# A two-layer decoder trunk: output projections one token half at a time, and the first MLP iteration's activations made product by product

## Chip, cores and metric

One core of one Trainium2 chip runs the whole program. The metric is device time in microseconds (us) of that core, from one execution; the median over three executions is compared. A profiled execution gives the trace that is read here.

## The reference

Two layers, each a mixer and an MLP, on 1024 tokens of width 1024 in fp32. What matters of it:

```python
# layer 0
y = concat([ssd_mixer(...), diff_attention(...)]) @ e_w_out      # 2048 -> 1024
# layer 1
y = concat([retention(...), sliding_window_attention(...)]) @ o_w_out   # 1536 -> 1024
def squared_relu_mlp(h, w1, w2):
    return square(relu(h @ w1)) @ w2                             # 1024 -> 4096 -> 1024
def sandwich(x, c_act, sublayer, g_pre, g_post, w_mod, b_mod):
    shift, scale, gate = split(c_act @ w_mod + b_mod, 3)
    h = rms_norm(x, g_pre) * (1 + scale) + shift
    return x + gate * rms_norm(sublayer(h), g_post)
```

Each layer runs `sandwich` twice, with the mixer and with the MLP. The normalisation is over a whole token row, so a token's `post` (gate, norm, residual) and the next `pre_norm` can begin only when every group of input columns has been projected for that token.

## The kernel before

**Numbers.** Each fp32 operand is split into a high part (a cast on ScalarE, line 156 for weights) and a low part (source minus high part, on VectorE, line 158). A product of two split operands is three matmuls: high by high, high by low, low by high. So every unit below is a run of triples of 128x512 matmuls on TensorE.

**Queues.** The program is written with tile pools, and a timeline scheduler sets the order of instructions on each engine from the order in the code, the buffers and its own estimates. Each engine then works strictly in that order: an instruction that waits holds up all that stand behind it. Weights arrive by DMA in `raw` (two buffers); the split parts `wh` and `wl` have four buffers each. `load_group` fetches one group of an output weight, 512 rows, as two 1 MB transfers and splits it into four blocks. Between them `bg` takes `bg_n` entries of a queue of background tasks (`bgq`): the modulation vectors of later sublayers, each a chain of four 1 MB loads and eight accumulations `macc` (line 299) on VectorE.

**Output projection.** `MixerOut` multiplies the mixer's result, which lies in DRAM (`yd`) by groups of 512 columns, with the output weight: four groups in layer 0, in the order 0, 1, 2, 3 (the first two SSD heads, the last two attention heads), and three in layer 1, in the order 2, 0, 1. Tokens come as 8 tiles of 128; tiles 0 to 3 are half 0, tiles 4 to 7 half 1. `half` loads a half group (`yr`), transposes it (`pyt`, four transposes for each of four blocks of 128 columns) and splits it (`u`). `out_unit` is one token tile by one 512-column half (`cc`) of the output: 12 matmuls (lines 466 to 468) into a bank `pg`, which VectorE then copies or adds into `Y` (lines 473 and 475). There are 8 units, 96 matmuls, in a half group.

The constructor runs half 0 of the first two groups while the second mixer of the layer (attention) goes on; `finish` then runs the rest. Before: half 1 of the second group, whose weights are still there, half 1 of the first group with its weights loaded again, and then each further group with both halves in one go. In the last group every tile's two units are followed by `post`, the `pre_norm` of the tile before, and from tile 5 on by `hT_cols` of half 0: the transposes `pht` that give the MLP its input, feature by token. The scheduler may bring rows of `finish` forward into the attention's last heads, which use the same engines: a block of 128 queries there goes score matmuls (`psc`) on TensorE, bias and row maximum on VectorE (line 1225), exponential on ScalarE, a weighted difference on VectorE (1238), transposes of the probabilities (`pat`, 1245), copies (1247), products with v (`pav`, 1251) and a normalisation (1255 to 1258).

**MLP.** `mlp` is a seven-product scheme over 2x2 blocks of the activations (half 0 and half 1 of the tokens, lower and upper 512 features) and of the weights. Each of eight iterations takes 256 columns of each weight half and runs products 1, 2, 4, 6, 7, 5, 3, each for two 128-column parts `g`, 12 matmuls (lines 557 to 559) per part. Products 1 and 2 use half 0 alone. In iteration 0, `second_half` turns half 1 (the transposes at line 574), makes the sums and differences and splits them, one quarter k after the other for all of products 4, 6, 7, 5, 3. `yp.whole` keeps half 0 in unsplit fp32 for it.

Of the kernel before, what the change touches and what calls it, by code (L numbers as in the profile page):

```python
# [9 lines left out]
F32 = mybir.dt.float32  # L10
F32R = mybir.dt.float32r
BF16 = mybir.dt.bfloat16
AF = mybir.ActivationFunctionType
# [15 lines left out]
def trunk(ctx: ExitStack, tc: tile.TileContext, x, c, rel_bias, norm_gains, mod_w, mod_b, mlp_w1, mlp_w2,  # L29
# [447 lines left out]
    def out_group(yp, us, blks, s, first, last):  # L477
        if not last:
            for cc in range(2):
                for t in range(NT):  # L480
                    out_unit(yp, us, blks, t, cc, first)
        else:
            xs = {}
            for t in range(NT):
                for cc in range(2):
                    out_unit(yp, us, blks, t, cc, first)
                xs[t] = post(yp, t, s)
                if s == sub_last:
                    continue
                if t:  # L490
                    pre_norm(yp, t - 1, xs[t - 1])
                if t == 5:
                    hT[0] = new_hT(0)
                    yp.whole = None
                    if s % 2 == 0:
                        pairs = [slot(17 + i, [P, 2, 512], F32, "whole") for i in range(3)]
                        pairs.append(const.tile([P, 2, 512], F32, tag="macc", name="whole"))
                        yp.whole = [t[:, i] for t in pairs for i in range(2)]
                if t >= 5:
                    k0 = (t - 5) * 3  # L500
                    hT_cols(yp, 0, s + 1, hT[0], range(k0, min(k0 + 3, 8)), yp.whole)
            if s != sub_last:
                pre_norm(yp, 7, xs[7])

                def second():
                    hT[1] = make_hT(yp, 1, s + 1)
                return second

# [4 lines left out]
    def mlp(yp, s):  # L513
# [19 lines left out]
        with ExitStack() as st:  # L533
# [27 lines left out]
            def second_half():  # L561
                a, b = mcol[s]
# [3 lines left out]
                for i, at_ in ((6, 8), (5, 4), (3, 0)):  # L566
                    A[i] = (of(pieces(at_)), of(pieces(at_ + 2)))
                for k in range(4):
                    a11, a12 = yp.whole[k], yp.whole[k + 4]
                    a2 = []  # L570
                    for kk, tag in ((k, "u3"), (k + 4, "c21")):
                        ps = pt.tile([P, 512], F32, tag="t", name="pht")
                        for i in range(4):
                            nc.tensor.transpose(ps[:, i * P:(i + 1) * P], yp.Y[4 + i][:, kk * P:(kk + 1) * P], ident)
                        a2.append(block(tag))
                        nc.scalar.activation(a2[-1], ps, AF.Identity, scale=a[:, kk:kk + 1], bias=b[:, kk:kk + 1])
                        if kk >= 4:
                            nc.scalar.activation(hh1[:, kk], ps, AF.Identity, scale=a[:, kk:kk + 1], bias=b[:, kk:kk + 1])
# [32 lines left out]
            for it in range(8):  # L611
# [11 lines left out]
                if it == 0:  # L623
                    second_half()
# [969 lines left out]
```

## Time and profile before

| what | value |
|---|---|
| median of 3 runs | 3029.69 us (3027.28 to 3030.26) |
| the profiled execution's own time | 3030.93 us |
| its span, first to last instruction | 3029.1 us |
| mean granted TensorE clock | 0.986 |
| TensorE busy | 97% of the span |
| VectorE busy | 66% |
| ScalarE busy | 43% |

The profiled execution took 1.24 us more than the median, and 1.8 us of its time lie outside the span. TensorE is busy nearly throughout, so the table alone says that few microseconds can be won; where its gaps are has to be read by place. Busy shares of the other engines are averages over stages that differ.

### The profile page before, as it was taken

To read this page: it belongs to the slowest core of one execution; us is meant where nothing else is said; L and a number is where in the kernel's file an instruction comes from. 1 tells how busy PE (TensorE), PEld (TensorE's weight loads), DVE (VectorE), ACT (ScalarE), POOL (GpSimd) and SP (SyncE) were. 2 spreads that over 40 slices of the span, in tenths; PEclk is the share of its full clock that TensorE was granted. 3 is DMA by queue.
4 is the path that set the end of the run, shared out by engine and by line. 5 is a ranking of instruction groups with operands and counts; after the bars stand their busy time and mean duration, and the time that the engine had idled before them with its cause. 6 is when DMAs were issued, how large, how long until landed. Compare 5 with 4: busy or idle time off the path is not lost.

```text
span 3029.1 us, 40060 instructions
## 1 busy us (share of the span) xinstructions
PE 2929.4 (97%) x15250; PEld 2471.4 (82%) x15250; DVE 1991.2 (66%) x3222; ACT 1309.4 (43%) x2348; POOL 474.2 (16%) x430
## 2 busy tenths in 40 slices
PE   8999999999999989999999989999999899999998
PEld 5888879888877867888888878989988678888887
DVE  5787885565586579876646845565454876666476
ACT  5232334555553264454433545432222644454333
POOL 0243443323210030000000232011101200000021
PEclk9999999999999999999999999999999999999999
DMA  6221311212142236646736542153242454476464
GB/s 215 75 89 57 120 53 46 66 41 61 46 150 71 89 127 217 221 163 235 290 125 226 191 134 63 33 168 101 84 153 77 140 188 162 153 260 231 151 223 166
DMA packets 268707, 413.59 MB, mean 137 GB/s; under 512 B 15337, under 2 KB 151138, under 8 KB 267618
## 3 DMA queue, kind: packets, MB, share of 16 engines
q1 hardware_dynamic: 268128, 410.92, 40.3%
q8 instruction: 120, 1.97, 0.3%
q14 instruction: 73, 0.60, 0.1%
q10 hardware_dynamic: 386, 0.11, 0.0%
HBM read 319.23 MB, written 91.75 MB: 136 GB/s over the span
## 4 chain that ended last, share of the span: by engine, by line
PE 81%; DVE 10%; DMA 4%; ACT 2%; issue 2%; POOL 1%; SPq 0%; POOLq 0%; DVEq 0%; ACTq 0%
PE pw L740 5%; PE pw L741 5%; PE pw L742 5%; PE pw L557 4%; PE pg L454 4%; PE pg L456 4%; PE pg L455 4%; PE pw L558 4%; PE pw L559 4%; PE pg L808 4%; PE pg L809 3%; PE pg L810 3%; PE pg L466 3%; PE pg L468 3%; PE pg L467 3%; PE pg L740 2%
## 5 line engine op out<-in xcount | busy, mean ns | idle before, releaser
L156 ACT CAST wh<-raw 128x1024 fp32r<-128x1024 f32 (+1 forms) x218 | 227.5, 1047 | 294.7 <-PE pw L558 97.7
L808 PE MATMUL pg<-wh,hh 128*128 128x256 f32 (+1 forms) x992 | 292.4, 295 | 18.5 <-DVE zs L843 10.6
L454 PE MATMUL pg<-hh,wh 128*128 128x512 f32 x736 | 292.8, 398 | 1.4 <-DVE ks L1340 0.8
L456 PE MATMUL pg<-hh,wl 128*128 128x512 f32 x736 | 291.9, 397 | 0.3 <-DVE ms L133 0.3
L455 PE MATMUL pg<-hl,wh 128*128 128x512 f32 x736 | 291.9, 397 | 0.0
L810 PE MATMUL pg<-wh,hl 128*128 128x256 f32 (+1 forms) x992 | 287.5, 290 | 0.6 <-DVE hl L439 0.6
L809 PE MATMUL pg<-wl,hh 128*128 128x256 f32 (+1 forms) x992 | 287.4, 290 | 0.0
L158 DVE TENSOR_TENSOR wl<-raw,wh 128x1024 fp32r<-128x1024 f32 (+1 forms) x162 | 199.3, 1232 | 130.3 <-ACT wh L156 127.4
L510 ACT CAST u<-uraw 128x1024 fp32r<-128x1024 f32 x112 | 117.1, 1049 | 299.8 <-PE pw L741 178.2
L511 DVE TENSOR_TENSOR u<-uraw,u 128x1024 fp32r<-128x1024 f32 x112 | 141.1, 1261 | 154.5 <-ACT u L510 153.7
L741 PE MATMUL pw<-wl,u 128*128 128x512 f32 x608 | 240.3, 395 | 0.0
L740 PE MATMUL pw<-wh,u 128*128 128x512 f32 x608 | 240.1, 396 | 0.0
L742 PE MATMUL pw<-wh,u 128*128 128x512 f32 x608 | 239.4, 394 | 0.0
L135 POOL TENSOR_TENSOR rs<-ms,expo 128x1 f32<-128x1 f32 x160 | 107.3, 671 | 682.2 <-DVE ms L133 664.2
L808 PEld LDWEIGHTS pg<-wh,hh 128*128 128x128 f32 x992 | 193.8, 195 | 21.9 <-DVE zs L843 10.3
L810 PEld LDWEIGHTS pg<-wh,hl 128*128 128x128 f32 x992 | 193.1, 195 | 2.5 <-DVE hl L439 1.3
L809 PEld LDWEIGHTS pg<-wl,hh 128*128 128x128 f32 x992 | 193.7, 195 | 1.8 <-issue 0.5
L466 PE MATMUL pg<-wh,u 128*128 128x512 f32 x448 | 181.9, 406 | 3.6 <-DVE u L940 3.1
L468 PE MATMUL pg<-wh,u 128*128 128x512 f32 x448 | 178.2, 398 | 0.0
L467 PE MATMUL pg<-wl,u 128*128 128x512 f32 x448 | 177.5, 396 | 0.0
L158 POOL TENSOR_TENSOR wl<-raw,wh 128x1024 fp32r<-128x1024 f32 x58 | 144.2, 2490 | 138.2 <-ACT wh L156 119.3
L454 PEld LDWEIGHTS pg<-hh,wh 128*128 128x128 f32 x736 | 139.1, 189 | 29.5 <-PE pg L456 1.2
(456 smaller groups left out, 7242.2 us busy)
## 6 DMA issues: line engine op xcount, KB each, us to landing
x<-in_mlp_w_dram SPq DMA_DIRECT2D x128, 512.0 KB, 6.6
uraw<-ud SPq DMA_DIRECT2D x56, 1024.0 KB, 5.5
raw<-in_mod_w_dram SPq DMA_DIRECT2D x24, 1024.0 KB, 5.0
ud<-sums SPq DMA_DIRECT2D x48, 512.0 KB, 4.2
raw<-in_mlp_w_dram SPq DMA_DIRECT2D x18, 1024.0 KB, 5.4
raw<-in_e_w_in_dram SPq DMA_DIRECT2D x32, 512.0 KB, 3.9
ud<-c SPq DMA_DIRECT2D x64, 256.0 KB, 3.1
mraw<-in_mod_w_dram SPq DMA_DIRECT2D x32, 512.0 KB, 4.9
```

Of the source, the lines that this page charges most:

```text
L158: lo_on[0].tensor_tensor(out=wl, in0=src, in1=wh.bitcast(F32), op=ALU.subtract)
L454: mm(ps, lhsT=wh[:, k], rhs=hh[:, k], start=(k == 0), stop=False)
L455: mm(ps, lhsT=wh[:, k], rhs=hl[:, k], start=False, stop=False)
L456: mm(ps, lhsT=wl[:, k], rhs=hh[:, k], start=False, stop=(k == 7))
L466: mm(ps, lhsT=uh[:, tl], rhs=wh[:, f % 2], start=(f == 0), stop=False)
L468: mm(ps, lhsT=ul[:, tl], rhs=wh[:, f % 2], start=False, stop=(f == 3))
L740: mm(ps[t], lhsT=uh[:, k, ts], rhs=wh[:, k], start=b, stop=False, **on)
L741: mm(ps[t], lhsT=uh[:, k, ts], rhs=wl[:, k], start=False, stop=False, **on)
L742: mm(ps[t], lhsT=ul[:, k, ts], rhs=wh[:, k], start=False, stop=e, **on)
L808: mm(ps[:, 0:n], lhsT=hh[:, k, tl], rhs=wh[:, i], start=(k == 0), stop=False)
L809: mm(ps[:, 0:n], lhsT=hh[:, k, tl], rhs=wl[:, i], start=False, stop=False)
L810: mm(ps[:, 0:n], lhsT=hl[:, k, tl], rhs=wh[:, i], start=False, stop=(k == 7))
```

## The change

Half 0 of all groups comes first, then half 1 of all groups. In `finish`, half 0 of the third (and fourth) group is projected next, tile by tile. Then the background queue is emptied, and half 1 is run for the groups in reverse order; the last group's weights are still there, the others are loaded again. Tiles 0 to 3 are complete by then, so a helper `along` puts their `post`, `pre_norm` and the eight `hT_cols` between the units of half 1. In the first group's half 1, which is now the last work of the projection, each tile's two units are followed by its `post` and `pre_norm`. `finish` calls `load_group` five times in a pass with four groups counting the constructor's two calls before, now seven; with three groups four before, now five. The half transposes in `finish` all take their bank from pool `pt`.

In iteration 0 of the MLP, `second_half` becomes a generator. It makes the operands of one product at a time, in the order 4, 7, 6, 5, 3, and product 6 comes behind product 7. The lower features of half 1 are turned twice (16 transposes and four scale-and-shift activations more in each MLP), in place in their bank. The buffers `u3` and `c21` hold a copy of the upper features, and the products' results live in `yp.whole`; the sums of iteration 0 go out in single DMAs. Iterations 1 to 7 are as before, but for the sign of one difference.

```diff
-    def out_group(yp, us, blks, s, first, last):
-        if not last:
-            for cc in range(2):
-                for t in range(NT):
-                    out_unit(yp, us, blks, t, cc, first)
...
+                a11, a12 = yp.whole[0:4], yp.whole[4:8]
+                a22 = [block(tag) for tag in ("u3", "c21") for _ in range(2)]
+
+                def turned(kk):
+                    ps = pt.tile([P, 512], F32, tag="t", name="pht")
+                    for i in range(4):
+                        nc.tensor.transpose(ps[:, i * P:(i + 1) * P], yp.Y[4 + i][:, kk * P:(kk + 1) * P], ident)
+                    return ps, dict(scale=a[:, kk:kk + 1], bias=b[:, kk:kk + 1])
+
+                def a21(k):
+                    ps, ab = turned(k)
+                    nc.scalar.activation(ps, ps, AF.Identity, **ab)
...
-                    a21, a22 = a2
-                    tt(out=hl1[:, k + 4], in0=a22, in1=hh1[:, k + 4].bitcast(F32), op=sub)
-                    tt(out=a11, in0=a11, in1=a21, op=sub)
-                    tt(out=a21, in0=a21, in1=a22, op=add)
-                    tt(out=a22, in0=a22, in1=a11, op=sub)
-                    tt(out=a12, in0=a12, in1=a22, op=sub)
-                    for i, src in ((6, a22), (7, a11), (5, a21), (3, a12)):
-                        split_to(A[i][0](k), A[i][1](k), src)
+                    ps, ab = turned(k + 4)
+                    nc.scalar.activation(hh1[:, k + 4], ps, AF.Identity, **ab)
+                    nc.scalar.activation(a22[k], ps, AF.Identity, **ab)
+                    tt(out=hl1[:, k + 4], in0=a22[k], in1=hh1[:, k + 4].bitcast(F32), op=sub)
+                yield
+                for k in range(4):
+                    tt(out=a11[k], in0=a21(k), in1=a11[k], op=sub)
+                    to(7, k, a11[k])
+                yield
+                for k in range(4):
+                    tt(out=a11[k], in0=a22[k], in1=a11[k], op=add)
+                    to(6, k, a11[k])
+                    tt(out=a12[k], in0=a12[k], in1=a11[k], op=sub)
+                yield
+                for k in range(4):
+                    tt(out=a22[k], in0=a21(k), in1=a22[k], op=add)
+                    to(5, k, a22[k])
+                yield
+                for k in range(4):
+                    to(3, k, a12[k])
+                yield
...
-                if it == 0:
-                    second_half()
...
+                more = second_half() if it == 0 else iter(range(5))
+                next(more)
                 for g in range(2):
                     product(pe[g], 4, w, g, True, True)
-                w = split_w(shape, t2)
-                pb = [bank(), bank()]
-                for g in range(2):
-                    product(pb[g], 6, w, g, True, True)
-                    tt(out=p1[g], in0=pb[g], in1=p1[g], op=add)
-                tt(out=x12, in0=x22, in1=x12, op=sub)
+
+                def six():
+                    w, pb = split_w(shape, t2), [bank(), bank()]
+                    for g in range(2):
+                        product(pb[g], 6, w, g, True, True)
+                        tt(out=p1[g], in0=pb[g], in1=p1[g], op=add)
+
+                if it:
+                    six()
+                next(more)
+                tt(out=x12, in0=x12, in1=x22, op=sub)
                 w = split_w(shape, x12)
                 pc_ = [bank(), bank()]
-                u3, c21 = [block("u3") for _ in range(2)], [block("c21") for _ in range(2)]
+                if it:
+                    u3, c21 = [block("u3") for _ in range(2)], [block("c21") for _ in range(2)]
+                else:
+                    u3, c21 = yp.whole[0:2], yp.whole[2:4]
+                    for g in range(2):
+                        product(pc_[g], 7, w, g, True, True)
+                    next(more)
+                    six()
...
-            yr = hp.tile([P, 2, 4, 512], F32, tag="hl1", name="yr")
-            room = (pg, "g") if self.s == 0 else (pt, "t")
-            for i in (1, 0):
-                nc.sync.dma_start(out=yr[:, i], in_=self.yd[self.order[i]][:, 4:8])
-                us = self.half(i, 1, [yr[:, i, t] for t in range(4)], u_tiles(), *room)
-                if i == 0:
-                    bg_n[0] = 2
-                    self.gb = load_group(self.w, self.order[0] * 512)
-                for cc in range(2):
-                    for t in range(4, 8):
-                        out_unit(yp, [None, us], self.gb, t, cc, i == 1)
-            n = len(self.order)
+            def group(i):
+                return load_group(self.w, self.order[i] * 512)
+
             for i in range(2, n):
                 bg_n[0] = 5
-                yr = hp.tile([P, 8, 512], F32, tag=("hh0", "hl0")[i % 2], name="yr")
-                nc.sync.dma_start(out=yr, in_=self.yd[self.order[i]])
-                us = [self.half(i, hf, [yr[:, hf * 4 + t] for t in range(4)], u_tiles(), pt, "t") for hf in range(2)]
-                gb = load_group(self.w, self.order[i] * 512)
-                late = out_group(yp, us, gb, self.s, False, i == n - 1)
-            return yp, late
+                yr = hp.tile([P, 4, 512], F32, tag=("hl1", "hh0")[i % 2], name="yr")
+                nc.sync.dma_start(out=yr, in_=self.yd[self.order[i]][:, 0:4])
+                us = self.half(i, 0, [yr[:, t] for t in range(4)], u_tiles(), pt, "t")
+                self.gb = group(i)
+                for t in range(4):
+                    for cc in range(2):
+                        out_unit(yp, [us, None], self.gb, t, cc, False)
+            while bgq:
+                bgq.popleft()()
+            xs, k_at = {}, [0]
+
+            def along(step):
+
+                if step < 4:
+                    xs[step] = post(yp, step, s)
+                if 1 <= step < 5 and s != sub_last:
+                    pre_norm(yp, step - 1, xs[step - 1])
+                if step == 5 and s != sub_last:
+                    hT[0] = new_hT(0)
+                    yp.whole = None
+                    if s % 2 == 0:
+                        pairs = [slot(17 + i, [P, 2, 512], F32, "whole") for i in range(3)]
+                        pairs.append(const.tile([P, 2, 512], F32, tag="macc", name="whole"))
+                        yp.whole = [t[:, i] for t in pairs for i in range(2)]
+                if step >= 6 and s != sub_last and step < 14:
+                    hT_cols(yp, 0, s + 1, hT[0], (step - 6,), yp.whole)
+
+            step = 0
+            for i in reversed(range(n)):
+                if (n - 1 - i) % 2 == 0:
+                    yr = hp.tile([P, 2, 4, 512], F32, tag="hl1", name="yr")
+                    for j in range(i, max(i - 2, -1), -1):
+                        nc.sync.dma_start(out=yr[:, j % 2], in_=self.yd[self.order[j]][:, 4:8])
+                us = self.half(i, 1, [yr[:, i % 2, t] for t in range(4)], u_tiles(), pt, "t")
+                gb = self.gb if i == n - 1 else group(i)
+                for t in range(4, 8):
+                    for cc in range(2):
+                        out_unit(yp, [None, us], gb, t, cc, i == n - 1)
+                        if step % 2 == 0 or n == 3:
+                            along(step if n == 3 else step // 2)
+                        step += 1
+                    if i == 0:
+                        x_new = post(yp, t, s)
+                        if s != sub_last:
+                            pre_norm(yp, t, x_new)
+
+            def second():
+                hT[1] = make_hT(yp, 1, s + 1)
+            return yp, second
```

On TensorE, at the end of layer 0's attention, before: the last query blocks of the last head (`psc`, `pat`, `pav`), with the units of half 1 of groups 1 and 0 (lines 466 to 468, `pg` from `u` and the weights).

```order
L1251 MATMUL pav<-v,aT 128x128 x6
L1245 MATMUL pat<-kmat,p 128x128 x4
L867 MATMUL psc_8800<-ks,qh 128x512
L868 MATMUL psc_8800<-ks,ql 128x512
L466 MATMUL pg<-wh,u 128x512
L467 MATMUL pg<-wl,u 128x512
L468 MATMUL pg<-wh,u 128x512
L466 MATMUL pg<-wh,u 128x512
L467 MATMUL pg<-wl,u 128x512
```

After, at the same place (the attention's lines are 882, 883, 1297 and 1303 now): the first row is the last matmul of the constructor's units.

```order
L468 MATMUL pg<-wh,u_9120 128x512
L1303 MATMUL pav<-v,aT 128x128 x3
L1297 MATMUL pat<-kmat,p 128x128 x4
L882 MATMUL psc_8840<-ks,qh 128x384
L883 MATMUL psc_8840<-ks,ql 128x384
L1297 MATMUL pat<-kmat,p 128x128 x2
L882 MATMUL psc_8800<-ks,qh 128x512
L883 MATMUL psc_8800<-ks,ql 128x512
L1303 MATMUL pav<-v,aT 128x128 x6
L1297 MATMUL pat<-kmat,p 128x128 x4
L882 MATMUL psc_8878<-ks,qh 128x256
L883 MATMUL psc_8878<-ks,ql 128x256
```

The 96 unit matmuls that stood among the last four query blocks have moved behind them; what is left there are the attention's own rows, down to the last `pav`, and then the transposes of the third group's half 0.

On VectorE, at the same place, after (`macc` is the modulation chain, 1277 the bias and maximum, 1290 the weighted difference, 1299 the copy, 1310 the normalisation):

```order
L1277 ISA psc_8840,mx<-psc_8840,bt_4027 128x384
L1277 ISA mx 128x1
L1277 ISA psc_8878,mx<-psc_8878,bt_4027 128x256
L1277 ISA mx 128x1
L299 SCALAR_TENSOR_TENSOR macc<-raw,cact,macc 128x1024
L1290 SCALAR_TENSOR_TENSOR p<-p,rc 128x512
L1285 RECIPROCAL rc<-mx 128x1
L133 TENSOR_SCALAR ms<-ssd__8791 128x1
L299 SCALAR_TENSOR_TENSOR macc<-raw,cact,macc 128x1024
L1287 TENSOR_SCALAR rc<-mx,rc,nlam 128x1
L1299 COPY aT<-pat 128x512
```

Four `macc` rows and one split of such a vector stand there now among the rows of the last query blocks; before, the first of these `macc` rows stood behind the last normalisation of the attention.

On TensorE, at the start of layer 0's MLP, before: rows of products 1 and 2 (557 to 559), the transposes of half 0 that are left (435) and the first of half 1 (574).

```order
L557 MATMUL pw<-hh_10327,wh 128x512
L435 MATMUL pht<-kmat,y_8948 128x128 x16
L558 MATMUL pg<-hl_10328,wh 128x512
L559 MATMUL pg<-hh_10327,wl 128x512
L557 MATMUL pg<-hh_10327,wh 128x512
...
L558 MATMUL pw<-hl_10328,wh 128x512
L559 MATMUL pw<-hh_10327,wl 128x512
L574 MATMUL pht<-kmat,Y 128x128 x8
L557 MATMUL pg<-hh_10327,wh 128x512
```

After (the products' lines are 525 to 527, the half 1 transposes 544; the first row is the last matmul of the projection):

```order
L468 MATMUL pg<-wh,u 128x512
L525 MATMUL pw<-hh_9981,wh 128x512
L526 MATMUL pw<-hl_9982,wh 128x512
L544 MATMUL pht<-kmat,Y 128x128 x2
L525 MATMUL pg<-hh_9981,wh 128x512
L526 MATMUL pg<-hl_9982,wh 128x512
...
L526 MATMUL pw<-hl_9982,wh 128x512
L527 MATMUL pw<-hh_9981,wl 128x512
L544 MATMUL pht<-kmat,Y 128x128 x4
L525 MATMUL pg<-hh_9981,wh 128x512
```

The transposes of half 0 no longer stand behind the first products; they are done among the units of half 1. Of half 1's transposes two stand already among the last units (not shown), two more after two matmuls of product 1, and the next ones behind 22 more.

## Rows read from the trace of the kernel before

**Rows 1.** The page's busy time of each engine: us (share of span) xinstructions.
```profile
PE 2929.4 (97%) x15250; PEld 2471.4 (82%) x15250; DVE 1991.2 (66%) x3222; ACT 1309.4 (43%) x2348; POOL 474.2 (16%) x430
```

**Rows 2.** Windows of 20 us: length, then busy time (and count) of each engine, clock.
```profile
core 0: us, PE busy (x) PEld busy (x) DVE busy (x) ACT busy (x) POOL busy (x), PEclk, DMA share, GB/s
...
940.00:960.00 20.00, 20.00 (x110) 17.06 (x108) 12.44 (x35) 6.96 (x21) 1.10 (x2) 1.00 0.04 11
...
960.00:980.00 20.00, 15.14 (x66) 11.94 (x66) 14.53 (x26) 7.74 (x16) 1.65 (x3) 0.83 0.48 155
...
1100.00:1120.00 20.00, 10.57 (x44) 7.77 (x42) 18.37 (x26) 13.97 (x22) 4.06 (x5) 0.72 0.31 106
...
1140.00:1160.00 20.00, 16.60 (x70) 12.67 (x69) 19.97 (x26) 8.23 (x12) 0.00 (x0) 1.00 0.60 193
...
2380.00:2400.00 20.00, 11.90 (x35) 9.11 (x36) 16.91 (x26) 14.18 (x24) 2.00 (x3) 0.66 0.23 79
```

**Rows 3.** TensorE in order of time, 966 to 979: start, length, idle before it.
```profile
969.58 1.31 PE L932 MATMUL pyt<-kmat,yr 128*128 128x128 f32 x8 [1.17 <-DVE u L940]
...
973.95 0.79 PE L466 MATMUL pg<-wh,u 128*128 128x512 f32 x1 [3.05 <-DVE u L940]
...
978.38 0.63 PE L467 MATMUL pg<-wl,u 128*128 128x512 f32 x1
```

**Rows 4.** Windows at the same place, columns as in rows 2.
```profile
970.00:972.00 2.00, 0.90 (x7) 0.42 (x4) 1.02 (x5) 1.34 (x2) 0.55 (x1) 1.00 1.04 377
...
974.00:976.00 2.00, 2.00 (x5) 1.61 (x6) 1.91 (x3) 0.00 (x0) 0.00 (x0) 0.50 0.35 124
```

**Rows 5.** VectorE in order of time, 938 to 973, columns as in rows 3.
```profile
938.75 0.70 DVE L1225 CUSTOM_DVE_ANT_0 psc<-psc,bt 128x512 f32<-128x512 f32 x1 [0.19 <-PE psc L868]
...
948.18 0.57 DVE L1225 CUSTOM_DVE_ANT_0 psc<-psc,bt 128x384 f32<-128x384 f32 x1
...
950.47 0.62 DVE L1238 SCALAR_TENSOR_TENSOR p<-p,rc 128x384 f32<-128x384 f32 x1
...
951.81 1.23 DVE L158 TENSOR_TENSOR wl<-raw,wh 128x1024 fp32r<-128x1024 f32 x1 [0.72 <-ACT wh L156]
...
960.15 0.30 DVE L1225 CUSTOM_DVE_ANT_0 psc<-psc,bt 128x128 f32<-128x128 f32 x1 [0.15 <-PE psc L868]
...
971.95 1.28 DVE L299 SCALAR_TENSOR_TENSOR macc<-raw,cact,macc 128x1024 f32<-128x1024 f32 x1 [0.56 <-DMA raw<-in_mod_w_dram]
```

**Rows 6.** The page's DMA issues: KB each, median us from issue to landing.
```profile
raw<-in_mod_w_dram SPq DMA_DIRECT2D x24, 1024.0 KB, 5.0
```

**Rows 7.** TensorE in order of time, 1107 to 1124, columns as in rows 3.
```profile
1107.39 0.79 PE L558 MATMUL pg<-hl,wh 128*128 128x512 f32 x1 [1.07 <-DVE hl L439]
...
1111.39 0.63 PE L559 MATMUL pw<-hh,wl 128*128 128x512 f32 x1
...
1119.60 0.69 PE L574 MATMUL pht<-kmat,Y 128*128 128x128 f32 x2 [4.51 <-DVE Y L382]
...
1122.22 0.47 PE L559 MATMUL pg<-hh,wl 128*128 128x512 f32 x1
...
1122.76 0.40 PE L558 MATMUL pg<-hl,wh 128*128 128x512 f32 x1
...
1123.00 0.40 PE L559 MATMUL pg<-hh,wl 128*128 128x512 f32 x1
```

**Rows 8.** VectorE in order of time, 1109 to 1119: token tile 7's chain.
```profile
1109.60 0.68 DVE L393 TENSOR_TENSOR yg<-Y,gg 128x512 f32<-128x512 f32 x1
...
1112.05 1.28 DVE L398 SCALAR_TENSOR_TENSOR xt<-yg,rs,xt 128x1024 f32<-128x1024 f32 x1 [0.45 <-POOL rs L135]
...
1118.79 0.75 DVE L382 TENSOR_SCALAR Y<-xt,rs 128x1024 f32<-128x1024 f32 x1 [0.73 <-POOL rs L135]
```

**Rows 9.** The page's groups: busy time, mean ns of one, idle time before.
```profile
L156 ACT CAST wh<-raw 128x1024 fp32r<-128x1024 f32 (+1 forms) x218 | 227.5, 1047 | 294.7 <-PE pw L558 97.7
...
L466 PE MATMUL pg<-wh,u 128*128 128x512 f32 x448 | 181.9, 406 | 3.6 <-DVE u L940 3.1
```

More of the change, by code (lines that the diff above doesn't have):

```diff
@@ L475, in out_unit @@
             nc.vector.tensor_tensor(out=dst, in0=ps, in1=dst, op=ALU.add)
-    def out_group(yp, us, blks, s, first, last):
-        if not last:
-            for cc in range(2):
-                for t in range(NT):
-                    out_unit(yp, us, blks, t, cc, first)
-        else:
-            xs = {}
-            for t in range(NT):
-                for cc in range(2):
[L486 to L507, printed above, removed]
     def split_to(hi, lo, src):
@@ new lines, in to @@
+                def to(i, k, src):
+                    split_to(A[i][0](k), A[i][1](k), src)
+                for k in range(4):
+                    ps, ab = turned(k + 4)
[6 more added lines that the diff above has]
+                    to(7, k, a11[k])
@@ L646, in mlp @@
                     square_relu(c21[g], c21[g])
+                if it == 0:
+                    next(more)
                 w = split_w(shape, x11)
@@ L652, in mlp @@
                     square_relu(u3[g], u3[g])
+                if it == 0:
+                    next(more)
                 w = split_w(shape, x22)
@@ L657, in mlp @@
                     square_relu(p1[g], p1[g])
-                sums = [slot(17 + i, [P, 2, 512], F32, "sums") for i in range(3)]
+                if it:
+                    sums = [slot(17 + i, [P, 2, 512], F32, "sums") for i in range(3)]
+                    by_g = [[t[:, g] for t in sums] for g in range(2)]
+                else:
+                    by_g = [[block("u3"), block("c21"), yp.whole[4 + g]] for g in range(2)]
                 for g in range(2):
@@ L662, in mlp @@
                     nc.sync.dma_start(out=ud[4][kt], in_=u3[g])
-                    tt(out=sums[0][:, g], in0=c21[g], in1=u3[g], op=add)
-                    tt(out=sums[1][:, g], in0=sums[0][:, g], in1=c11[g], op=sub)
+                    s0_, s1_, s2_ = by_g[g]
+                    tt(out=s0_, in0=c21[g], in1=u3[g], op=add)
+                    tt(out=s1_, in0=s0_, in1=c11[g], op=sub)
                     tt(out=c21[g], in0=c11[g], in1=c21[g], op=sub)
                     nc.sync.dma_start(out=ud[7][kt], in_=c21[g])
-                    tt(out=sums[2][:, g], in0=p1[g], in1=sums[1][:, g], op=sub)
+                    tt(out=s2_, in0=p1[g], in1=s1_, op=sub)
                     nc.sync.dma_start(out=ud[2][kt], in_=p1[g])
                 for i, n in ((5, 0), (6, 1), (3, 2)):
-                    nc.sync.dma_start(out=ud[i][2 * it:2 * it + 2].rearrange("k p n -> p k n"), in_=sums[n])
+                    if it:
+                        nc.sync.dma_start(out=ud[i][2 * it:2 * it + 2].rearrange("k p n -> p k n"), in_=sums[n])
+                    for g in range(0 if it else 2):
+                        nc.sync.dma_start(out=ud[i][g], in_=by_g[g][n])
                 if it:
@@ L946, in finish @@
             yp.Y[0:4] = self.Y
+            s, n = self.s, len(self.order)
             def u_tiles():
                 return [yp.u() for _ in range(4)]
-            yr = hp.tile([P, 2, 4, 512], F32, tag="hl1", name="yr")
-            room = (pg, "g") if self.s == 0 else (pt, "t")
-            for i in (1, 0):
-                nc.sync.dma_start(out=yr[:, i], in_=self.yd[self.order[i]][:, 4:8])
-                us = self.half(i, 1, [yr[:, i, t] for t in range(4)], u_tiles(), *room)
-                if i == 0:
-                    bg_n[0] = 2
-                    self.gb = load_group(self.w, self.order[0] * 512)
-                for cc in range(2):
-                    for t in range(4, 8):
-                        out_unit(yp, [None, us], self.gb, t, cc, i == 1)
```

14 lines of the change are left out of this document (3 added, 11 removed).

## The prediction

> **What bounds the kernel now.** I read the busy times first: TensorE is busy 2929.4 us of the span, 97% [rows 1]. A change can thus matter in two ways: it adds or removes work on TensorE, or it opens or closes gaps there. So next I read windows of 20 us for TensorE's busy time and clock, and looked for short ones near the lines of the diff. From 940 to 960 TensorE is busy 20.00 of 20 us, though this is the end of layer 0's attention, whose own work is slow on VectorE and ScalarE. From 960 to 980 it is busy 15.14 at a clock of 0.83. At the start of layer 0's MLP, 1100 to 1120, it is 10.57 at 0.72, and 1140 to 1160 still 16.60; layer 1's MLP has 11.90 at 0.66 in 2380 to 2400 [rows 2]. These are the two places of the change: the hand-over from attention to output projection, and that from projection to MLP.
>
> Last I read both places in order of time. In the first, TensorE waits 1.17 and 3.05 us for the split halves u, and then runs multiplies slowly: the eleven from 973.95 to 978.38 start 0.44 us apart, where 1122.76 to 1123.00 gives 0.24 [rows 3, 7]. The granted clock shows why: 1.00 in 970 to 972, 0.50 in 974 to 976, after a gap; those are 2.4 and 1.2 GHz [rows 4]. In the second, TensorE waits longest, 4.51 us, for the Y of the last token tile, and runs at half from 1107.39 to 1111.39 and again until 1122.22 [rows 7].
>
> **The end of layer 0's attention.** What it costs before: 4.86 us of idle time in 960 to 980 (20 minus 15.14), and about 12 multiplies at half, each 0.2 us longer, 2.3 us. Together 7.2.
>
> The change takes 96 multiplies from between the last four query blocks; at 0.23 us they are 22 us of work that filled TensorE while VectorE went through its chain. They are not lost, they run later; but now nothing stands in the order between the attention's own rows. So the stretch lasts as long as VectorE's chain. I sum that chain from the order of the change, from the last unit on, with a length for each row from [rows 5] less 0.05 to 0.1 us of overlap with its follower: seven bias-and-maximum rows (0.57 for 384 wide, 0.70 for 512, 0.30 for 128) 2.8; four weighted differences (0.62 for 384) 1.9; four copies 1.7 and six normalisations 2.0, priced as rows of their width; two lower weight parts (1.23) 2.3; one add into Y 0.6; four macc rows (1.28) 4.8 and one split of that kind 1.1; some twenty small ones 2.4. That is 19.6 us. The macc rows read 1 MB loads that take 5.0 us [rows 6] with two buffers, so the third waits; with the waits for ScalarE in the last block I add 3.4. So 23 us. A check from the trace: the bias rows of the last blocks start at 938.75 and 960.15, three blocks apart [rows 5], 7.1 us a block; three and a half blocks make 25.
>
> TensorE's own work in it is some 48 small transposes and products, 0.11 to 0.16 us each (eight in 1.31 [rows 3]), and 14 score matmuls; I take 7.6 us. Idle are thus 15.4. After it the first units wait for their halves, pair by pair, 1.5 us (0.70 for each of VectorE's two rows); the multiplies then start at half clock, 2.3 as before; and I take 2.0 for the small matmuls inside the chain that run at half, as [rows 4] shows it behind a gap of 3 us. Sum 21.2, so **+14** against 7.2.
>
> Bounds: without the macc rows and their waits in the chain (they might be hidden in ScalarE's time) it is 14 us, idle 6.4, with 1.5, 2.3 and 1 some 11, so +4. With 25 us and 5.0 more of waits for the loads, and all the 7.6 us at half, 32, so +24. I stand nearer the middle, since the order puts the macc rows in front of the weighted differences.
>
> A page's rule stands beside this. The Trainium skill, "TensorE: Matmul & The Clock Gate", section "HAM oscillation — how this bites in real kernels", says that gaps without matmuls let the clock fall, and that each stretch behind such a gap starts cold and pays again; by it the tail's small matmuls would all be cold, and the sum 5.6 us higher, 3043 (a rival below). The drop to 0.50 in [rows 4] agrees with it; the 1.00 of 970 to 972, in which TensorE is busy 0.90 of 2.00 us, shows that a half idle stretch alone did not do it here.
>
> Layer 1's attention ends as before in the order: the constructor's units still lie between its rows. I take nothing there.
>
> **The start of each MLP.** Before, layer 0: 9.43 us idle in 1100 to 1120, 3.40 in 1140 to 1160 [rows 2], and 16 multiplies at half between 1107.39 and 1122.22, 3.1 us. Together 15.9. The cause is one chain: the last tile's `post` and `pre_norm` begin on VectorE at 1109.60 and its Y is ready at 1119.54 [rows 8], behind the half 0 transposes and their activations.
>
> After the change, half 0 is turned while half 1 is projected, and VectorE can begin with tile 7 when its last unit ends. That moment I call E. The chain has the same links, 9.9 us by [rows 8], and 0.3 for the add before it: Y is ready at E + 10.2. TensorE has product 1 in front, 24 multiplies at 0.23, 5.5 us, and a few transposes: 5.9. It waits 4.3. Product 2's bank is that of product 1, which ScalarE must copy first; there it stands behind casts of 1.05 us [rows 9], and I take 1.5. Half clock behind this gap costs 1.6 (8 multiplies at 0.2). Then product 4, 7, 6 and 5 advance quarter by quarter as VectorE delivers; each operand is two or three rows of 0.6 us, against 12 multiplies in 2.8, and waits before 6 and 5 I put at 3.6. The 16 added transposes cost 16 times 0.11, 1.8. Sum 12.8, so **-3** in each MLP. Layer 1's has the same pattern [rows 2], so -6 for both. Bounds: if products 2 to 5 wait nowhere the loss is 7, a gain of 9; if VectorE (it is busy 18.37 and 19.97 of 20 us in these windows [rows 2]) falls behind by one operand per product, 6 us more, a loss of 3.
>
> **Weights loaded again, smaller edits.** Three more `load_group` calls in all, 2 MB each, with 12 casts and 12 subtractions. All of it lies beside multiplies: a half group is 96 of them, 22 us. What could surface is a boundary: with tiles outside and column halves inside, all four blocks of a group are used till its last unit, and the first buffer comes free 18 multiplies, 4.2 us, before the group's end. A cast of 1.05 [rows 9] and a subtraction of 1.23 [rows 5] fit in it with 1.9 to spare, as long as neither engine is behind. If that cover is gone, each of six boundaries costs up to 2 us. The units' group shows only 3.6 us of idle time over 448 rows before [rows 9]; I take 0, with bounds 0 and 12. Single DMAs in place of pairs, the sums' new places, the changed sign and the bank's pool: 0, since the sums are waited for only by the second half of the MLP, over 100 us later. The activations of the added transposes, in place, are counted above with the chain of product 7.
>
> **Sum.** 3030.9 (the profiled time) + 14 - 6 + 0 = 3038.9; that execution lies 1.2 above the median, so **3038**.
>
> **Rivals.**
> *Tail covered, hand-overs better (faster).* The macc rows don't hold up the chain, tail +4 and no lasting half clock; and product 1 with the units' transposes covers tile 7's chain, so that products 2 to 5 wait nowhere: 9 back in each MLP. For it speaks that VectorE's work is ordered by product now and that transposes of half 0 have left the path. Against it, tile 7's chain of 9.9 us is longer than product 1. 3030.9 + 4 - 18 - 1.2 = 3015.7; with a tail of +9, 3020.7, which is the number I give it. The place is the wait before product 1's follower; it decides when the two gains together exceed the tail by over 6 us. Chance 0.14.
> *They cancel.* Tail +8, because the accumulations find their loads there and the chain is 17 us, and 3.5 gained in each MLP: 3030.9 + 8 - 7 - 1.2 = 3030.7. Chance 0.30.
> *Half clock throughout the tail.* All 7.6 us of small matmuls take 15.2, 5.6 more than I counted: 3043. Against it stands the 1.00 of 970 to 972 at less than half busy [rows 4]. Chance 0.07. The Trainium skill, "TensorE: Matmul & The Clock Gate", the section named above, points to this rival.
> *Weights late.* 2 us at six boundaries, 12: 3050. VectorE would have to be behind at each one. Chance 0.05.
>
> **How the numbers follow.** The forecast has 0.44. 0.2% is 6.1 us and about what a measurement of this kernel can tell from no change: faster ends at 3023.6, slower begins at 3035.7. Faster is the first rival, 0.14. Within it fall the second, 0.30, and the low end of the forecast (tail +11 or less), 0.04: 0.34. Slower: 0.40 of the forecast, 0.07 and 0.05: 0.52. The forecast's own range is 3033 to 3045. The range reaches down over the second rival and up over the third, 3025 to 3047, and leaves out the first and the last, 0.19.
>
> **What the profile would show.** The tail: a window of 23 us before the third group's units in which TensorE is busy about 8 us (15 of idle time more than in 940 to 960), released by VectorE and with macc rows among the attention's. If TensorE there is busy over 14 of 23 us, the chain was overestimated. The hand-over: idle of 3 to 6 us behind product 1, released by Y, and no wait for half 0's `hh` and `hl`. No wait over 1 us at the units' first rows of a reloaded group. I would be wrong most easily in the tail: by what the loads of the macc rows cost, or if the gaps there turn out to be fillable after all; next by products 7 and 6, if VectorE runs behind there.

## The result, and the profile after

The changed kernel takes 3046.84 us (median of 4, 3044.55 to 3047.88) against 3029.75 before: ratio 1.0057, interval 1.0040 to 1.0074. It is slower by 17 us, where 8 were forecast. The profiled execution took 3046.58, its span is 3044.8.

Four stages hold the difference. Their borders are the first matmul of product 1 in each MLP and the first matmul of the MLP's second weight behind it; the last 329.4 to 330.4 us hardly differ between the kernels here.

| kernel (profiled execution) | start to MLP 0 | MLP 0, first weight | to MLP 1 | MLP 1, first weight |
|---|---|---|---|---|
| before | 1098.5 | 327.4 | 946.2 | 327.6 |
| changed | 1109.7 | 330.4 | 947.7 | 327.4 |
| difference | +11.2 | +3.1 | +1.5 | -0.2 |

TensorE's rows are the same in all kernels here up to a pair of `pat` transposes; each profiled execution reaches that pair at another time, between 896.4 and 900.9 us. So the first column is better counted from there: 199.7 us before, 210.5 in the changed kernel, +10.8; the other 0.4 comes from ahead of it. And 18 transposes, about 2 us, have moved in each layer from the MLP's column to the one before it. Without them layer 0's projection loses about 9 us, the MLPs 5 and 2, and layer 1's projection nothing.

Windows of 20 us of the changed kernel, columns as in [rows 2], at the end of layer 0's attention, then at the start of its MLP and of layer 1's:

```profile
940.00:960.00 20.00, 15.61 (x60) 12.15 (x61) 14.86 (x44) 7.70 (x25) 4.78 (x6) 0.55 0.28 91
960.00:980.00 20.00, 19.52 (x90) 15.86 (x89) 9.91 (x17) 3.33 (x5) 0.00 (x0) 0.94 0.71 263
...
1120.00:1140.00 20.00, 16.66 (x71) 13.45 (x72) 10.38 (x14) 15.43 (x24) 0.55 (x1) 0.76 0.31 105
1140.00:1160.00 20.00, 14.90 (x69) 10.53 (x67) 20.00 (x32) 15.16 (x24) 0.00 (x0) 1.00 0.47 158
1160.00:1180.00 20.00, 18.68 (x70) 15.09 (x71) 19.80 (x24) 6.25 (x10) 0.00 (x0) 0.83 0.50 136
...
2420.00:2440.00 20.00, 13.65 (x59) 9.85 (x59) 20.00 (x33) 12.58 (x20) 0.00 (x0) 0.92 0.47 159
```

Where [rows 2] had 20.00 busy at a clock of 1.00, 940 to 960 has 15.61 at 0.55. Shorter windows there:

```profile
936.00:940.00 4.00, 2.92 (x22) 2.29 (x21) 3.25 (x9) 2.27 (x7) 0.33 (x1) 1.00 0.96 347
940.00:942.00 2.00, 1.52 (x10) 1.20 (x11) 2.00 (x8) 0.00 (x0) 1.13 (x1) 0.96 0.47 178
942.00:950.00 8.00, 5.77 (x24) 4.49 (x23) 7.84 (x24) 4.06 (x13) 1.91 (x2) 0.50 0.43 140
950.00:958.00 8.00, 6.32 (x23) 4.81 (x24) 3.76 (x16) 2.96 (x11) 1.75 (x4) 0.50 0.12 35
958.00:962.00 4.00, 4.00 (x14) 3.31 (x14) 1.45 (x3) 1.37 (x2) 0.00 (x0) 0.50 0.51 129
```

Without the units TensorE is not mostly idle, as I had it: from 936 to 958 it is busy 16.5 of 22 us. But from 942 on it works at the half level (0.50, 1.2 GHz), so its work fills the time. The fall comes without one long gap: no idle time between 932 and 958 is over 0.92 us. It comes among these three waits, in TensorE's order of time:

```profile
938.79 0.33 PE L1297 MATMUL pat<-kmat,p 128*128 128x128 f32 x1 [0.32 <-ACT aT L1299]
939.88 0.44 PE L882 MATMUL psc<-ks,qh 128*128 128x384 f32 x1 [0.76 <-ACT p L1280]
940.98 1.75 PE L1303 MATMUL pav<-v,aT 128*128 128x128 f32 x10 [0.48 <-DVE aT L1299]
```

I use one measure for the clock: over windows of 1 us, busy time times what the clock lacks of 1.00. From 930 to 980 it gives 8.3 us, before (960 to 1000) 2.5. Idle time from 845 to MLP 0 is 11.5 us after, 9.8 before. So layer 0's tail, the end of its attention, lost 5.8 us to the clock and 1.7 to gaps.

At MLP 0, TensorE in order of time, the waits over half a microsecond:

```profile
1122.30 0.69 PE L544 MATMUL pht<-kmat,Y 128*128 128x128 f32 x2 [5.99 <-DVE Y L382]
1124.03 0.80 PE L525 MATMUL pg<-hh,wh 128*128 128x512 f32 x1 [1.04 <-ACT p L607]
...
1153.64 0.50 PE L526 MATMUL pg<-s,wh 128*128 128x512 f32 x1 [1.30 <-DVE s L479]
1157.18 0.50 PE L526 MATMUL pg<-s,wh 128*128 128x512 f32 x1 [1.87 <-DVE s L479]
1161.32 0.79 PE L525 MATMUL pg<-hh,wh 128*128 128x512 f32 x1 [2.94 <-DVE p L628]
```

The waits for half 0 and the 4.51 of [rows 7] are gone, as forecast. In their place stand 5.99 for Y, and 6.1 in three waits at product 6 and for the bank that its sum releases. With them goes half clock of 6.0 us (before 4.2), behind the first gap and again behind the 2.94. MLP 1 has the same five waits (6.00, 1.04, 1.27, 1.88, 2.94).

### The profile page after: what moved, and what is told of

Same layout as the page of the kernel before. It is cut to its first block, busy times and chain, and to the rows that moved or that the text cites. A ratio compares the mean times of both kernels' runs of the same rounds, so it can differ in the third digit from the quotient of the medians.

```text
span 3044.8 us, 40207 instructions
## 1 busy us (share of the span) xinstructions
PE 2942.4 (97%) x15282; PEld 2479.5 (81%) x15282; DVE 2002.2 (66%) x3235; ACT 1326.3 (44%) x2367; POOL 480.2 (16%) x430
## 4 chain that ended last, share of the span: by engine, by line
PE 83%; DVE 9%; DMA 3%; ACT 2%; issue 2%; POOL 1%; SPq 0%; POOLq 0%; ACTq 0%; DVEq 0%
PE pw L755 5%; PE pw L756 5%; PE pw L757 5%; PE pw L525 4%; PE pw L526 4%; PE pw L527 4%; PE pg L454 4%; PE pg L456 4%; PE pg L455 4%; PE pg L823 4%; PE pg L824 3%; PE pg L825 3%; PE pg L466 3%; PE pg L467 3%; PE pg L468 3%; PE pg L525 2%
## 5 line engine op out<-in xcount | busy, mean ns | idle before, releaser
L156 ACT CAST wh<-raw 128x1024 fp32r<-128x1024 f32 (+1 forms) x230 | 239.9, 1047 | 283.2 <-PE pw L526 95.1
L823 PE MATMUL pg<-wh,hh 128*128 128x256 f32 (+1 forms) x992 | 292.5, 295 | 17.9 <-DVE zs L858 10.6
L158 DVE TENSOR_TENSOR wl<-raw,wh 128x1024 fp32r<-128x1024 f32 (+1 forms) x174 | 211.5, 1220 | 141.4 <-ACT wh L156 126.7
```

Source lines behind the costliest of these rows:

```text
L158: lo_on[0].tensor_tensor(out=wl, in0=src, in1=wh.bitcast(F32), op=ALU.subtract)
L823: mm(ps[:, 0:n], lhsT=hh[:, k, tl], rhs=wh[:, i], start=(k == 0), stop=False)
```

## The experiments

All were compared with the kernel before on the same chip. A ratio's interval is 95%. Stages are from one profiled execution each.

**One: the bank pool.** The predicted 0 for the pool was the easiest term to test.

```diff
-us = self.half(i, 0, [yr[:, t] for t in range(4)], u_tiles(), pt, "t")
+us = self.half(i, 0, [yr[:, t] for t in range(4)], u_tiles(), *((pg, "g") if s == 0 and i == 2 else (pt, "t")))
```

> The changed kernel with one word of it altered: in layer 0, half 0 of the third group is transposed in a bank of pool pg, not of pool pt, which the attention uses. Theory: the tail's cost comes from the pool. With a bank of its own the group's 96 multiplies go back among the attention's last query blocks, TensorE stays at a clock of 1.00 there, and the about 8 us of the tail (1.3 more of idle time and 6 of half clock by the two traces) come back: 3036 to 3041. Rival, that of the prediction: the pool costs nothing and the tail is lost because half 1 was moved; then the time stays at 3045 to 3048.

3040.65 us, ratio 1.0031 (1.0020 to 1.0043): 6 us faster than the changed kernel. Windows and one row of TensorE:

```profile
940.00:960.00 20.00, 19.28 (x100) 16.38 (x101) 15.58 (x39) 5.28 (x17) 1.44 (x2) 1.00 0.48 167
960.00:980.00 20.00, 10.76 (x53) 8.16 (x52) 11.07 (x27) 5.72 (x13) 1.67 (x4) 0.83 0.37 135
...
979.89 1.94 PE L947 MATMUL pyt<-kmat,yr 128*128 128x128 f32 x8 [7.44 <-DMA yr<-ye]
```

The multiplies are back among the last query blocks and the clock stays at 1.00 there: the tail was lost by the pool. (The kernel before took `pg` in layer 0 for its first two half groups in `finish`.) From the common pair of rows to MLP 0 it is 207.4 us, 3.1 of the 6 us; 2.1 more lie in MLP 0, whose code is the same but whose half clock took 4.1 instead of 6.0. A new wait takes part of the gain, 7.44 us for the fourth group's half 0. The last head's blocks end with the tokens of half 0, so its load cannot start earlier.

**Two and three: the halves of the change.** The projection of the change with the whole MLP of before (below against the changed kernel, at its core), and the reverse, with the `finish` and `out_group` of before.

```diff
-more = second_half() if it == 0 else iter(range(5))
-next(more)
+if it == 0:
+    second_half()
...
```

> The new projection order with the MLP of before. Theory: the tail costs 8 as in the changed kernel, and each MLP start is about as before, with half 0's transposes out of it but tile 7's chain and the all-at-once operands still to wait for: 3036 to 3041, and the rest of the 17 us lies in the MLP part. Rival: the projection order carries all of the loss, 3045 to 3048.

> The projection of before with the new first MLP iteration. Theory: the tail is as before and the product-by-product order costs its 16 added transposes (1.8 us) and waits before products 6 and 5 in each MLP: 3032 to 3038. Rival, that of the prediction: the product order gains about 3 in each MLP, 3022 to 3028.

Projection only: 3028.74, ratio 0.9994 (0.9985 to 1.0003), no change. MLP only: 3044.4, ratio 1.0048 (1.0035 to 1.0061); its profiled execution was one of the longer ones, 3049.4. All four numbers that were expected of these two runs missed. By stage, in the table's order: projection only 1107.5, 322.8, 948.8, 319.3; MLP only 1101.1, 335.4, 948.0, 333.7.

So the new projection order loses 10.6 at the tail, counted from the common pair (210.3 against 199.7), and gains 4.6 and 8.3 in the MLPs, the 2 us of moved transposes in all three. The new MLP iteration, put on this, costs 7.7 in MLP 0 (330.4 less 322.8) and 8.1 in MLP 1; put on the projection of before, it costs 8.0 and 6.1.

Where that goes is seen on VectorE. Two windows of 20 us from the last tile's Y on, first the changed kernel, then projection only:

```profile
1122.16:1142.16 20.00, 18.76 (x81) 15.00 (x82) 11.25 (x15) 15.43 (x24) 0.00 (x0) 0.81 0.24 79
1142.16:1162.16 20.00, 13.64 (x60) 9.72 (x60) 20.00 (x33) 13.00 (x21) 0.00 (x0) 0.95 0.47 158
```

```profile
1119.91:1139.91 20.00, 18.82 (x80) 15.26 (x81) 17.86 (x27) 16.72 (x28) 0.00 (x0) 0.81 0.24 79
1139.91:1159.91 20.00, 17.80 (x79) 13.94 (x78) 19.99 (x27) 8.97 (x13) 0.00 (x0) 1.00 0.57 184
```

VectorE is busy 11.25 us in the first window of the changed kernel and 17.86 in that of the other, and full in both second windows: in the changed kernel 6.6 us of its work come late. The changed kernel's VectorE in order of time shows the hole:

```profile
1127.18 0.69 DVE L559 TENSOR_TENSOR hl<-u,hh 128x512 fp32r<-128x512 f32 x1 [0.64 <-ACT u L558]
1133.21 1.23 DVE L158 TENSOR_TENSOR wl<-raw,wh 128x1024 fp32r<-128x1024 f32 x1 [5.34 <-PE pht L544]
```

Two turned blocks stand ahead of product 2, and the next ones behind its 24 multiplies. By products, the first two blocks (upper features of two quarters) feed two rows on VectorE; all at once, the first two (lower and upper features of one quarter) feed nine.

**Four: product 2 in banks of its own**, so that it need not wait for the copy of product 1 and stands ahead of the wait for Y.

```diff
+p2 = pa if it else [bank(), bank()]
 for g in range(2):
-    product(pa[g], 2, w, g, False, True)
-    square_relu(c11[g], pa[g])
+    product(p2[g], 2, w, g, it == 0, True)
+    if it == 0:
+        tt(out=c11[g], in0=p2[g], in1=p1[g], op=add)
+    square_relu(c11[g], c11[g] if it == 0 else pa[g])
```

> The changed kernel, but in iteration 0 product 2 has banks of its own and is added to product 1 on VectorE, so that its 24 multiplies need not wait for ScalarE's copy and stand ahead of the transposes that wait for tile 7's Y. If that wait (6.0 us, with 1.04 behind it and about 2.5 us of half clock) bounds the MLP start, each MLP gains 6 to 8: 3031 to 3035. If VectorE, busy 20.00 of 20 us behind it, sets the pace of products 4, 7, 6, 5, 3, the waits only move to them: 3043 to 3047.

3036.61, ratio 1.0023 (1.0014 to 1.0032), between the two. MLP 0 takes 326.4, MLP 1 324.0, 4.0 and 3.3 less than in the changed kernel:

```profile
1119.99 0.44 PE L544 MATMUL pht<-kmat,Y 128*128 128x128 f32 x2 [1.04 <-DVE Y L382]
1123.83 0.80 PE L525 MATMUL pw<-hh,wh 128*128 128x512 f32 x1 [3.40 <-ACT hh L557]
...
1155.88 0.80 PE L525 MATMUL pw<-s,wh 128*128 128x512 f32 x1 [2.94 <-DVE p L631]
```

Of the 7.0 us in the first two waits 4.4 remain, most of them now at product 4's operands; the three later waits keep their length (1.29 and 1.87 stand between). So neither theory holds alone. The rest of the run's gain, 2.3, lies before MLP 0, but half of it ahead of the common pair, where TensorE's rows are the same. From the pair it is 209.3 us, 1.1 less than in the changed kernel: the tail's clock loss is 5.6 there, with nearly the same rows in a slightly other order.

**Seven: work off VectorE.** Low parts of products 7 and 3 and the differences for 3 go to GpSimd, 12 rows in each MLP.

```diff
-split_to(A[i][0](k), A[i][1](k), src)
+split_to(A[i][0](k), A[i][1](k), src, nc.gpsimd if i in (7, 3) else None)
-tt(out=a12[k], in0=a12[k], in1=a11[k], op=sub)
+nc.gpsimd.tensor_tensor(out=a12[k], in0=a12[k], in1=a11[k], op=sub)
```

> The changed kernel with the low parts of product 7 and 3 and the differences for product 3 of iteration 0 on GpSimd, which is idle there: VectorE has 12 rows of 36 less in each MLP. Theory: products 7, 6 and 5 wait for VectorE, whose queue by products is too long (20.00 of 20 us busy); their waits of 1.3, 1.9 and 2.9 us and the half clock behind them shrink: 3036 to 3042. Rival: ScalarE's casts and activations are as late, or GpSimd is slower than what it replaces: 3045 to 3050.

3045.59, ratio 1.0058 (1.0044 to 1.0072): as the changed kernel. In the 20 us behind Y VectorE is busy 10.38, and MLP 0 takes 331.0. So the forecast gain is not there, but the run does not tell whether VectorE's queue is too long, for VectorE was hardly relieved. A GpSimd row of this size takes 1.30 to 2.20 us against 0.69, and beside it VectorE's own rows grew:

```profile
1144.39 0.68 DVE L571 TENSOR_TENSOR u<-pht,u 128x512 f32<-128x512 f32 x1
1145.58 1.75 POOL L568 TENSOR_TENSOR whole<-whole 128x512 f32<-128x512 f32 x1
1146.10 1.78 DVE L566 TENSOR_TENSOR whole<-c,whole 128x512 f32<-128x512 f32 x1
1147.80 1.79 DVE L479 TENSOR_TENSOR s<-u,s 128x512 fp32r<-128x512 f32 x1
```

Eight rows of lines 566 and 479 took 1.02 to 1.83 us in each MLP; in the changed kernel all rows of these lines there take 0.68 to 0.70. The twelve rows that left VectorE were some 7 us, and these eight added about 7.

**Nine: three products by quarters.** Two loops are joined, so that a quarter's blocks feed products 4, 7 and 6.

```diff
     tt(out=hl1[:, k + 4], in0=a22[k], in1=hh1[:, k + 4].bitcast(F32), op=sub)
-yield
-for k in range(4):
     tt(out=a11[k], in0=a21(k), in1=a11[k], op=sub)
     to(7, k, a11[k])
-yield
-for k in range(4):
     tt(out=a11[k], in0=a22[k], in1=a11[k], op=add)
     to(6, k, a11[k])
     tt(out=a12[k], in0=a12[k], in1=a11[k], op=sub)
 yield
+yield
+yield
```

> The changed kernel with two loops joined: the operands of products 4, 7 and 6 are made quarter by quarter (all three of a quarter, then the next), those of 5 and 3 behind them as in the change. Theory: with products one by one VectorE has only one row for each pair of transposes behind the last Y (busy 11.3 us in the 20 us behind it, against 17.9 with the MLP of before), and its 36 rows end that much later; with six rows for each quarter it is busy 14 us or more there, the waits of 1.3, 1.9 and 2.9 us and the half clock behind the last shrink, and each MLP gains 2 to 4: 3038 to 3043. Rival: the loss is the 16 added transposes, their activations and the sums read from a PSUM bank, whatever the order; then 3045 to 3048.

3035.83, ratio 1.0024 (1.0014 to 1.0035): 11 us back. MLP 0 takes 324.7 and MLP 1 323.3, 5.8 and 4.0 less, though all 16 transposes are still there.

```profile
1123.14:1143.14 20.00, 18.82 (x81) 15.18 (x82) 15.42 (x21) 15.35 (x25) 0.00 (x0) 0.83 0.24 79
...
1155.67 0.50 PE L526 MATMUL pg<-s,wh 128*128 128x512 f32 x1 [1.20 <-DVE s L479]
1158.68 0.50 PE L525 MATMUL pg<-hh,wh 128*128 128x512 f32 x1 [1.81 <-DVE p L626]
```

VectorE is busy 15.42 there, the three waits of 6.1 are two of 3.0, and the clock loss of MLP 0 is 2.8 instead of 6.0. The order by products is thus shown as the main cause: VectorE does the same 36 rows, and only gets blocks to work on earlier. 1.9 and 4.0 us against projection only remain for the added transposes, their activations and what is still by products (5 and 3).

**Eight: no macc rows in the tail**, by one word at the third group's load; the tasks run when the queue is emptied.

```diff
-bg_n[0] = 5
+bg_n[0] = 0 if i == 2 and n == 4 else 5
```

> The changed kernel without background tasks at the third group's load: the four macc rows and the split of that vector leave the attention's tail and run later, when the queue is emptied. The prediction's sum had 5.9 us of these rows and 3.4 of waits in the chain. If VectorE's chain sets the tail, it gets 4 to 6 us shorter: 3040 to 3044. If the chain goes through the query blocks' own links (scores, exponential, transposes, products), the rows are beside it and the time stays within 2 of 3046.8.

3041.6, ratio 1.0043 (1.0030 to 1.0056), 5 us less than the changed kernel, as the first theory had it; the profiled execution, 3043.85, is 2.7 less. Behind the constructor's last unit, the first `pav` and the third group's first unit on TensorE, the changed kernel first, then this run:

```profile
932.02 0.83 PE L1303 MATMUL pav<-v,aT 128*128 128x128 f32 x6
958.29 0.78 PE L466 MATMUL pg<-wh,u 128*128 128x512 f32 x1
```

```profile
932.10 0.83 PE L1303 MATMUL pav<-v,aT 128*128 128x128 f32 x6
953.72 0.78 PE L466 MATMUL pg<-wh,u 128*128 128x512 f32 x1
...
1005.65 1.45 PE L947 MATMUL pyt<-kmat,yr 128*128 128x128 f32 x8 [1.76 <-issue]
```

The tail takes 21.6 us instead of 26.3. So the rows were in the chain, and without them it is 4.7 shorter, where the sum had 9.3 for them (5.9 and 3.4). The idle time in the tail is nearly the same (6.3 and 6.9), the clock loss is not: how much of the 4.7 the rows took themselves and how much the half clock they brought, the run does not tell apart. Only 1.4 us of it arrive at MLP 0 (209.1 against 210.5 from the common pair), since a new wait of 1.76 stands at 1005.65, with half clock behind it. 1.8 us lie in MLP 0, again as half clock (4.3 instead of 6.0).

**Five and six: a version that beats both.** From the runs above: the projection by halves, the MLP of before, pool pg for the third group's half 0, and its half 1 right behind it under the same weights, as cover for the fourth group's load. `along` goes one step with every unit then.

```diff
+early = i == 2 and n == 4
...
+if early:
+    us = self.half(i, 1, [yr[:, 4 + t] for t in range(4)], u_tiles(), pt, "t")
+    for t in range(4, 8):
+        for cc in range(2):
+            out_unit(yp, [None, us], self.gb, t, cc, True)
...
-for i in reversed(range(n)):
+rest = [i for i in reversed(range(n)) if n == 3 or i != 2]
```

> The projection by halves with the MLP of before, the third group's half 0 in a bank of pool pg, and that group's half 1 (its weights are still there) right behind it, before the fourth group's half 0. Theory: the 7.44 us that the pool's change leaves open is the fourth group's half 0 waiting for its own load, since the last head's query blocks end with the tokens of half 0; 96 multiplies (22 us) in between hide it. Of the projection-only kernel's tail (11.1 us idle, 8.4 half clock from 845 on) some 8 to 12 come back: 3017 to 3022. Rival: the wait only moves, the tail gains no more than the pool's change alone did: 3023 to 3027.

3021.64, ratio 0.9973 (0.9962 to 0.9985): 8 us faster than the kernel before, 25 than the changed one. The windows of the tail:

```profile
940.00:960.00 20.00, 19.69 (x102) 16.72 (x103) 15.58 (x39) 4.86 (x17) 1.45 (x2) 1.00 0.19 60
960.00:980.00 20.00, 16.92 (x81) 13.13 (x80) 10.32 (x26) 4.84 (x13) 1.65 (x3) 0.91 0.39 145
```

The wait of 7.44 is gone. MLP 0 starts at 1101.6 and takes 321.0, MLP 1 319.8: the projection's gain in the MLPs is kept, and its loss at the tail is not.

The sixth adds experiment four's banks to this.

> The kernel of the run before (cover) with banks of its own for product 2 of iteration 0. If the wait for tile 7's Y (6.00 with 1.04 behind it and 2 to 3 us of half clock) can be filled by product 2's multiplies under the MLP of before too, each MLP gains 3 to 5, 7 to 9 below the run before. If VectorE's all-at-once operands set the pace, it is the same within 2.

3024.31, ratio 0.9987 (0.9978 to 0.9995), no gain. The wait for Y shrinks from 6.00 to 1.04 here too, but 3.40 and 2.08 come behind it, and the clock loss of MLP 0 is 5.2 instead of 2.3: as I read it (no run tells it apart), with the MLP of before product 2 was work that ran while VectorE filled its first quarters.

## Why the prediction was wrong, step by step

*What bounds the kernel* was right: all differences lie at the two hand-overs and in the clock behind them.

*The tail, +14.* Without the moved transposes it is about 9, inside the bounds. The chain's length was near (25 us from 932 to 957, forecast 23), but by luck: the background rows and their waits are worth at most 4.7 by experiment eight, half clock included, not 9.3, and without them some 21 us are left, not the 14 of the lower bound, for the query blocks' own links are longer. TensorE's work in it was undercounted: the sum took 48 small matmuls, the trace has 69 (48 products with v and 21 transposes), and with the 14 score matmuls they are 12.2 us at full clock, not 7.6. Idle are 6.5 us from 932 to 957, where the sum had 15.4, and the prediction's own sign against its chain came true: TensorE is busy 18.5 of these 25 us. The clock, 2.3 and 2.0 in the sum, took 8.3. The 2.0 were also counted twice, since in a stretch as long as VectorE's chain slower matmuls only fill waits that the 15.4 already holds; and the upper bound adds up to 34, or +27, not to 32. The rival of half clock throughout came near to what happened, with 0.07; the 1.00 of [rows 4] that spoke against it covered 2 us, the stretch here 20. The Trainium skill, "TensorE: Matmul & The Clock Gate", section "HAM oscillation — how this bites in real kernels", tells of TensorE's clock falling to half behind gaps without matmuls. The half clock is in the trace (0.50 from 942 to 962), but no long gap stands before it: no wait between 932 and 958 is over 0.92 us.

*The bank's pool, 0.* Wrong; the reason given for the 0 holds for the sums alone. The pool is what moved the multiplies, and one word of it gives 6 us back.

*The MLPs, -3 each.* This is the step that failed most. Without the moved transposes they came out at +5 and +2. Product 1's cover and the wait for Y were near (5.99 for 4.3, and 1.04 for 1.5), the 16 transposes were counted. But three waits of 6.1 stand where the sum had 3.6, and the clock loss is 6.0 and 4.9 where it had 1.6. I let the products advance at the pace of VectorE's rows, and did not look at what those rows wait for: product 2's multiplies stand between the first two turned blocks and the next, and leave VectorE idle for 5.34 us. With three products by quarters 5.8 and 4.0 us came back. And I put one number on two edits: the projection order gave the MLPs 4.6 and 8.3 (2 of each are moved transposes), the order by products took 7.7 and 8.1.

*Weights loaded again, 0.* Right. In layer 0 TensorE idles 0.2 us from 980 to MLP 0; layer 1's column has +1.5 with about 2 us of moved transposes in it.

Sum of the errors, without the moved transposes: -5.2 at the tail, +8.1 and +4.8 in the MLPs, -0.5 between them and 0.4 from ahead of the tail make 7.6, the distance from the 8.0 forecast to the 15.6 of the profiled executions. That 3046.84 still lies within 3025 to 3047 is luck: the tail came out lower than forecast and hid part of what the MLPs cost.

What stays open: why the clock fell at 942 with waits that short, and why experiment four's nearly equal rows lost 2.7 us of clock less there. About 1 us of the tail's 10.8 is neither half clock nor a gap nor moved transposes.

## What to carry to other kernels

Price an order of operands by what it feeds the engine that sets the pace: two turned blocks gave VectorE two rows or nine, and the loss appeared 20 us later at another engine. When work is to fill another stage's gaps, see that it takes no buffer from that stage's pool; here that decided whether it was placed there at all. And cost the two halves of a change apart, each against the kernel before: here one gained and the other took it back.

## What was not expected of the hardware

TensorE's granted clock stood at 0.50 for 20 us (942 to 962) in which the engine was busy 16.1 of 20 and no gap was as long as 1 us. It came back within the first run of multiplies without waits (0.92 in 962 to 964).

```profile
962.00:964.00 2.00, 2.00 (x12) 1.63 (x11) 0.70 (x1) 0.36 (x1) 0.00 (x0) 0.92 0.97 406
```

GpSimd took 1.30 to 2.20 us for a 128x512 fp32 row of two operands, where VectorE took 0.69. While it did so, VectorE's own rows on two operands in SBUF took up to 1.83 us; its rows that read the turned block from its bank (`pht`) stayed at 0.68 to 0.69 (experiment seven).
